# Output projection of a gated two-branch layer, in Strassen's form over four row tiles

## The chip, the cores and the metric

The kernel runs on one core of one Trainium2 chip. The metric is device time in microseconds of one execution, taken as the median over runs. Of the core's engines, PE does the matrix products, DVE, ACT and POOL work on whole rows of elements, and SP issues the transfers between DRAM and the on-chip memory (SBUF). Products are summed in PSUM, which holds eight banks of 512 float32 columns on 128 partitions. Each engine runs its own list of instructions in order; a semaphore is what one engine waits on for another.

## The reference

One layer on 1024 positions of width 1024. What matters here is the middle of it:

```python
merged = (sigmoid(g_a) * (y_att @ w_oa) + sigmoid(g_b) * (y_sgu @ w_ob))
x = x + merged @ w_out
x = x + conv_gated_mlp(rmsnorm(x, ffn_norm), w_up, conv_w, conv_b, w_down)
```

`g_a`, `g_b` are columns of the layer's input projection, `y_att` and `y_sgu` the two branches (attention and spatial gating, 512 wide each), `w_out` is 1024 x 1024, and the MLP projects up to 2 x 2816 columns, filters along the positions, gates, and projects down.

## The kernel before, in words

Everything is kept transposed: features on partitions in tiles of 128, positions along the free axis, whose halves are `L` (0 to 511) and `H` (512 to 1023). Each float32 operand of a product is split into a high part of PE's reduced-precision float32 type and the remainder; a product of two operands is three matmuls (high by high, high by low, low by high). The high part is written by ACT (`copy_hi`, L77), the remainder by DVE or POOL as a subtraction.

The program from the gates on is written out by hand: the order of the calls is the order of the instructions on every engine. Its stages:

1. **Gates** (`gate_pair`, one call for each of 8 column tiles). Both gate tiles of one number are four blocks, and their product by the normalized input is done in Strassen's form: seven products of 12 matmuls (`Blocks.prod`, L928 before, L933 after) for eight. `Left` holds the weight side of a pair: `load_p`, `load_q` fetch it, `sum_s1` to `sum_s4` add blocks on POOL, `split_p`, `split_q`, `split_s3`, `split_r` make high and low parts (`ph`, `pl`, `qh`, `ql`, `s3h`, `s3l` and `AX` in the trace). Beside the gates, `sums_step` makes in advance two sums of blocks of the MLP's up weights: load, two DVE additions (`ls`), store to DRAM. Loads run one step ahead through two buffers.
2. **Branches** (`branch`, 16 jobs of 24 matmuls into `po`). A job's result is multiplied with tanh values that come back from DRAM (`th`), the two branches are added to `m`, and `m_split` makes its parts. Ten more sums steps sit here. `run_jobs` runs all jobs: it issues the matmuls of job i, starts the weight load of job i+4, splits the weights of job i+2 (`wjh` by ACT, `wjl` by POOL), and then runs the rest of job i. `wjh` and `wjl` have two buffers each.
3. **Output projection** (`out_tile`, 8 jobs of 48 matmuls into `px`, one for each tile of 128 features of the result). After a job: the residual is added (`ac`, L1244), scaled rows `h` are made (L1246), `x2` goes to DRAM for the end of the program, and the blocks that the MLP's Strassen form needs (`B11`, `T1`, `B21`, `B22`, `T3`) are split tile by tile; `T2` and `T4` are kept raw. Squares are summed in `sq2` for the second norm.
4. **MLP**, 22 pairs of up columns (`first_pair`, then `fast_pair`), each seven products of 12 matmuls, with the filter and the gate of the pair before on DVE and ACT. The second norm's statistics (`ssq_cols`, 16 matmuls of 2 columns) are made in the first pair, and its row factor `rstd_b` (`rms_rows`, 4 matmuls of 512 columns) in the second, since it scales the results and not the operands. The down projection (`mlp`) is Strassen's form again, one product M at a time over four row tiles: the sums `X` and `Z` stay in PSUM, and a finished one is read out between products.

PSUM tiles of 1024 columns are handed out in rotation from four places (`PS`); a tile's place is free again when its last reader is done, and a wait covers the whole tile, not its halves.

## Time and profile before

| | |
|---|---|
| median of 3 runs (lowest, highest) | 1202.59 us (1201.78, 1203.99) |
| the profiled execution's own time | 1202.22 us |
| its span, first to last instruction | 1200.4 us |
| PE, DVE, ACT, POOL busy in the span | 99%, 74%, 45%, 47% |
| mean granted TensorE clock | 0.997 |

A span is the time from the first to the last recorded instruction. A matmul's record ends when its result is out, so records of neighbours overlap: 389 ns for one of 512 columns, while the next one starts 0.227 us after it. "Idle before" is time in which an engine had nothing running just ahead of an instruction, and the name after the arrow is what ended it.

### The profile page before, as it was taken

To read this page: it belongs to the slowest core of one execution; us is meant where nothing else is said; L and a number is where in the kernel's file an instruction comes from. 1 tells how busy PE (TensorE), PEld (TensorE's weight loads), DVE (VectorE), ACT (ScalarE), POOL (GpSimd) and SP (SyncE) were. 2 spreads that over 40 slices of the span, in tenths; PEclk is the share of its full clock that TensorE was granted. 3 is DMA by queue.
4 is the path that set the end of the run, shared out by engine and by line. 5 is a ranking of instruction groups with operands and counts; after the bars stand their busy time and mean duration, and the time that the engine had idled before them with its cause. 6 is when DMAs were issued, how large, how long until landed. Compare 5 with 4: busy or idle time off the path is not lost.

```text
span 1200.4 us, 15782 instructions
## 1 busy us (share of the span) xinstructions
PE 1183.8 (99%) x5850; PEld 1000.2 (83%) x5850; DVE 886.7 (74%) x1019; ACT 540.5 (45%) x839; POOL 569.3 (47%) x361
## 2 busy tenths in 40 slices
PE   8999999999999999999999999999999999999998
PEld 8889989888888888888788888888888888888886
DVE  7688966755648665668797878878887798866674
ACT  8456566744335222234444444344444445434331
POOL 2366684587768322344856665756666551000000
PEclk9999999999999999999999999999999999999999
DMA  7110133127686997342142333324333358965471
GB/s 274 31 53 19 54 124 131 36 100 244 244 313 212 351 323 270 134 158 106 45 150 88 123 116 121 127 91 143 105 132 107 104 200 273 395 227 193 151 237 60
DMA packets 78989, 191.01 MB, mean 159 GB/s; under 512 B 8896, under 2 KB 9152, under 8 KB 78912
## 3 DMA queue, kind: packets, MB, share of 16 engines
q1 hardware_dynamic: 78912, 190.00, 45.6%
q8 instruction: 46, 0.75, 0.3%
q14 instruction: 31, 0.25, 0.1%
HBM read 139.38 MB, written 50.59 MB: 158 GB/s over the span
## 4 chain that ended last, share of the span: by engine, by line
PE 87%; DVE 5%; ACT 1%; DMA 1%; issue 1%; POOL 0%; SPq 0%; ACTq 0%; DVEq 0%
PE pz L928 45%; PE pd L1634 10%; PE pdy L1634 7%; PE px L82 2%; PE po L83 2%; PE po L82 2%; PE px L83 2%; PE px L81 2%; PE po L81 2%; PE pvs L81 1%; PE pvs L83 1%; PE pvs L82 1%; PE pq L81 1%; PE pq L83 1%; PE pq L82 1%; DMA ls<-wup 1%
## 5 line engine op out<-in xcount | busy, mean ns | idle before, releaser
L928 PE MATMUL pz<-T,qh 128*128 128x512 f32 x480 | 148.0, 389 | 0.0
L887 POOL TENSOR_TENSOR pl<-lp,ph 128x1024 fp32r<-128x1024 f32 x30 | 72.9, 2430 | 86.3 <-ACT ph L77 86.1
L928 PE MATMUL pz<-B,ph 128*128 128x512 f32 x352 | 109.5, 392 | 0.0
L928 PEld LDWEIGHTS pz<-T,qh 128*128 128x128 f32 x480 | 90.0, 188 | 18.6
L928 PE MATMUL pz<-T,ql 128*128 128x512 f32 x240 | 93.4, 389 | 0.0
L98 POOL TENSOR_TENSOR wjl<-wj,wjh 128x512 fp32r<-128x512 f32 (+1 forms) x24 | 40.8, 1701 | 95.5 <-ACT wjh L77 95.5
L887 POOL TENSOR_TENSOR ql<-lq,qh 128x1024 fp32r<-128x1024 f32 x29 | 74.7, 2574 | 9.1 <-ACT qh L77 9.1
L928 PEld LDWEIGHTS pz<-B,ph 128*128 128x128 f32 x352 | 65.4, 188 | 15.5 <-ACT x L1482 1.9
L943 DVE TENSOR_TENSOR pz<-pz,rstd_b 128x1024 f32<-128x1024 f32 x60 | 73.9, 1232 | 4.6 <-ACT rstd_b L132 2.6
L887 POOL TENSOR_TENSOR s3l<-s,s3h 128x512 fp32r<-128x512 f32 x30 | 40.7, 1358 | 72.4 <-ACT s3h L77 72.4
L928 PE MATMUL pz<-T,s3h 128*128 128x512 f32 x240 | 73.9, 389 | 0.0
L928 PE MATMUL pz<-B,pl 128*128 128x512 f32 x176 | 68.6, 390 | 0.0
L1634 PE MATMUL pd<-bh,ah 128*128 128x512 f32 x176 | 68.5, 389 | 0.0
L1634 PE MATMUL pd<-bh,al 128*128 128x512 f32 x176 | 68.5, 389 | 0.0
L1634 PE MATMUL pd<-bl,ah 128*128 128x512 f32 x176 | 68.5, 389 | 0.0
L928 PE MATMUL pz<-T,AX 128*128 128x512 f32 x264 | 65.1, 397 | 0.0
L928 PE MATMUL pz<-B,AX 128*128 128x512 f32 x264 | 63.4, 389 | 0.0
L928 PEld LDWEIGHTS pz<-T,AX 128*128 128x128 f32 x264 | 50.6, 192 | 10.7
L928 PEld LDWEIGHTS pz<-B,AX 128*128 128x128 f32 x264 | 49.5, 188 | 10.3
L1340 DVE SCALAR_TENSOR_TENSOR tg<-pz,cp,tg 128x1023 f32<-128x1023 f32 (+1 forms) x44 | 56.2, 1278 | 0.8
L1340 DVE SCALAR_TENSOR_TENSOR tv<-pz,cp,tv 128x1023 f32<-128x1023 f32 (+1 forms) x44 | 56.2, 1277 | 0.8
L77 ACT ACTIVATE qh<-lq 128x1024 fp32r<-128x1024 f32 (+1 forms) x31 | 32.0, 1036 | 54.5 <-issue 25.4
(331 smaller groups left out, 3523.8 us busy)
## 6 DMA issues: line engine op xcount, KB each, us to landing
ls<-wup SPq DMA_DIRECT2D x22, 512.0 KB, 5.5
sum<-ls SPq DMA_DIRECT2D x22, 512.0 KB, 4.6
lp<-wup SPq DMA_DIRECT2D x22, 512.0 KB, 3.6
ra<-wdown SPq DMA_DIRECT2D x44, 256.0 KB, 4.8
b<-T SPq DMA_DIRECT2D x44, 256.0 KB, 3.9
B<-tv SPq DMA_DIRECT2D x33, 256.0 KB, 2.0
T<-tt SPq DMA_DIRECT2D x33, 256.0 KB, 2.0
b<-B SPq DMA_DIRECT2D x33, 256.0 KB, 3.9
```

What stands on the lines that cost most here:

```text
L77: return nc.scalar.activation(dst, src, AF.Copy, scale=scale)
L81: nc.tensor.matmul(out, wh, mh, start=first, stop=False, **kw)
L82: nc.tensor.matmul(out, wh, ml, start=False, stop=False, **kw)
L83: nc.tensor.matmul(out, wl, mh, start=False, stop=last, **kw)
L98: nc.gpsimd.tensor_tensor(l[:, :nk, :], r[:, :nk, :], h[:, :nk, :].bitcast(F), op=ALU.subtract)
L887: nc.gpsimd.tensor_tensor(l, r, h.bitcast(F), op=ALU.subtract)
L928: nc.tensor.matmul(o, p[:, k, :], y[:, q, k, :], start=not more and k == 0 and j == 0, stop=k == 3 and j == 2, skip_group_check=True)
L943: nc.vector.tensor_tensor(z, z, rstd_b, op=ALU.mult)
L1340: nc.vector.scalar_tensor_tensor(t[:, j:], p[:, 0:1024 - j], cw[:, ci, 2 - j:3 - j], t[:, j:], op0=ALU.mult, op1=ALU.add)
L1634: nc.tensor.matmul(o[d], p[:, k - k0, m], q[:, k - k0, :], start=new and k == 0 and j == 0, stop=k == HK - 1 and j == 2, skip_group_check= ...
```

## The change

`w_out` and the merged rows are each taken as four blocks, and the output projection becomes seven products M1, M2, M6, M5, M3, M7, M4, each over four row tiles and all of K = 512. A product is two groups (`out_group`) of 24 matmuls, so 14 groups take the place of the 8 tiles. `X` and `Z` are two PSUM tiles each, four row tiles of 512 columns. M1 is computed into `X` and copied to `Z`; M6, M5, M3 go on adding to `X`, M2 to `Z`; then M7 starts `Z` anew and M4 adds to it. The quarters of the result are `C11` (Z after M2), `C21` (X after M6, and Z after M4), `C22` (X after M5, and Z after M7) and `C12` (X after M3).

The sums of blocks of `w_out` are made in the gates' stage in eight steps of four DVE additions of 256 columns (`osum_step`), stored to DRAM (`wS`) and read back by the groups. `step` runs these eight first, then the 22 sums of the MLP: two steps in the first gate pair that had none, three in each later pair (two before), and one in each of the first ten branch jobs.

The merged rows stay whole in `m`, and their blocks `mB11`, `mB21`, `mB22`, `mT1` to `mT4` are summed and split after the branches and between the groups (`out_work`). The quarters' own work stands there too: adding the residual (`rows_add`), scaling (`rows_done`), splitting (`right_split`), squaring into PSUM and adding up (`squares`). The scaled rows no longer hold the first norm's factor. `first_pair` has its products in another order, leaves the statistics to the second pair, and takes its PSUM tiles where `X` was.

```diff
     def job_load(i):
         if i < len(jobs):
             src, nk, _ = jobs[i]
-            job_w[i] = wload(src, "wj", nk) if nk else first_left()
-            if not nk:
+            if nk == "g":
+                job_w[i] = raw("wj")
+                nc.sync.dma_start(job_w[i].rearrange("p (a b) m -> p a (b m)", a=2), src())
...
+    def osum_load(i):
+        if i < 8:
+            k, e = divmod(i, 2)
+            x = osum[i] = pools["ls"].tile([128, 4, 256], F, tag="ls", name=nm("os"), bufs=2)
+            for j in range(2):
+                nc.sync.dma_start(x[:, 2 * j:2 * j + 2],
+                                  a["wout"][:, k + 4 * j, :].rearrange("p (r m) -> p r m", r=2)
+                                  [:, :, 256 * e:256 * e + 256])
+        else:
+            sums_load()
+
+    def osum_step(i):
+        osum_load(i + 1)
...
+        sub(nc.vector, x[:, 3], x[:, 3], x[:, 1], ALU.add)
+        sub(nc.vector, x[:, 1], x[:, 0], x[:, 1])
+        sub(nc.vector, x[:, 0], x[:, 3], x[:, 0])
+        sub(nc.vector, x[:, 2], x[:, 2], x[:, 0])
+        nc.sync.dma_start(wS[:, :, k, 256 * e:256 * e + 256], x)
...
         gate_out(("b", c - 1), prev.zg)
-        if c > 1:
-            sums_step()
+        step()
         q.prod(q.v0, "S3", "T3")
...
         if nx:
             nx.sums_r()
-        if c > 1:
-            sums_step()
+        step()
         q.prod(q.v0, "A22", "T4", more=True)
...
+        if c > 1:
+            step()
         q.prod(q.v1, "S2", "T2")
         q.sums(x1, x7, q.v0)
...
-            if n % 2 == 0 or n in (5, 9):
-                sums_step()
+                block_split("B11" if c < 4 else "B21", slice(c % 4, c % 4 + 1), m[:, L].unsqueeze(1))
+                if c > 3:
+                    lo = ms[0][:, c - 4, :]
+                    sub(nc.vector, lo[:, L], lo[:, H], lo[:, L])
+                    sub(nc.vector, lo[:, H], m[:, H], lo[:, H])
+            if sums["make"] < NPAIR:
+                step()
...
+    def out_work(i):
+        hu = hx2["u"] if "u" in hx2 else None
+        if i == 0:
+            block_half("B22", 1, H)
+        if i == 1:
+            for d in range(4):
+                nc.scalar.copy(Z[d], X[d])
+            for k in range(0, 4, 2):
+                sub(nc.vector, ms[1][:, k:k + 2, H], ms[1][:, k:k + 2, H], ms[0][:, k:k + 2, L])
+            block_half("T2", 1, H)
+        if i == 2:
+            block_half("T1", 0, L)
+            block_half("T3", 0, H)
+        if i == 3:
+            rows_add("C11", Z)
+            for k in range(0, 4, 2):
+                sub(nc.vector, ms[1][:, k:k + 2, L], ms[1][:, k:k + 2, L], ms[1][:, k:k + 2, H])
+            block_half("T4", 1, L)
+        if i == 4:
+            hu = hx2["u"] = U("hu", F, [128, 2, 4, 512])
+            rows_done("C11", hu[:, 0])
+            right_split("B11", hu[:, 0], nc.gpsimd)
+            squares("C11", Z)
+        if i == 5:
+            rows_add("C21", X)
+        if i == 6:
+            rows_load("C12")
+        if i == 7:
+            rows_add("C22", X)
+        if i == 9:
+            rows_add("C12", X)
+            rows_done("C12", hu[:, 1])
+            right_sum(hu[:, 0], hu[:, 1], hu[:, 0])
+            right_split("T1", hu[:, 0], nc.gpsimd)
+            squares("C12", X)
+        if i == 11:
+            hc = pools["hc"]
+            rows_add("C22", Z)
+            rows_done("C22", hc)
+            right_split("B22", hc, nc.gpsimd)
+            right_sum(hu[:, 1], hc, hu[:, 1])
+            right_sum(hu[:, 0], hc, hu[:, 0])
+            right_split("T3", hu[:, 1], nc.vector)
+        if i == 12:
+            lefts[0].split_s3()
+            lefts[0].sums_r()
+            lefts[0].split_r(0)
+            right_split("T2", hu[:, 0], nc.vector)
+            squares("C22", X)
+        if i == 13:
+            lefts[0].split_q()
+            rows_add("C21", Z)
+            rows_done("C21", hu[:, 1])
+            right_split("B21", hu[:, 1], nc.vector)
+            right_sum(pools["hc"], hu[:, 1], hu[:, 0])
+            right_split("T4", pools["hc"], nc.vector)
...
+            o = Z if s in ("M2", "M7", "M4") else X
+            y = mb[RHS[s]]
+            for k in range(2):
+                for d in range(4):
+                    for j, (p, q) in enumerate(((0, 0), (0, 1), (1, 0))):
+                        nc.tensor.matmul(o[d], w[p][:, 4 * k + d, :], y[:, q, k0 + k, :],
+                                         start=s in ("M1", "M7") and k0 + k == 0 and j == 0,
+                                         stop=k0 + k == 3 and j == 2, skip_group_check=True)
             yield
...
+            out_work(i)
+        jobs.append((lambda: out_src(s, k0), "g", main))
```

In `squares`, ACT writes the square of a row tile into the PSUM half `o[d]`, and DVE adds that half to `sq2`. `first_pair` now runs A11 B11, S3 T3, S4 B22, S1 T1, S2 T2, A12 B21, A22 T4; `fast_pair`, for the second pair, runs A11 B11, then `ssq_cols`, S1 T1, `rms_rows`, and the rest.

How the change places the instructions, at three places. In the rows `wjh` and `wjl` are the parts of a job's weights, `mB`, `mT` blocks of the merged rows (`mB_623` is B22, `mT_627` T2, `mT_631` T1, `mT_632` T3, `mT_636` T4), `px_4923` and `px_4924` the two tiles of X, `px_4925` and `px_4926` those of Z.

ACT at the start of the projection, as it was (the work after the first two tiles):

```order
L77 ACTIVATE wjh_4926<-wj_4717 128x1024 [waits DMAHW6_49,PE_49,Pool_49]
L77 ACTIVATE B_616_4778<-h_4931 128x512 [waits DVE_49]
L77 ACTIVATE T_617_4779<-h_4931 128x512 [waits DVE_49]
L1263 ACTIVATE sq_4785<-ac_4871 128x1024
L77 ACTIVATE wjh_4993<-wj_4756 128x1024 [waits DMAHW0_49,PE_49,Pool_49]
```

and as it is now (after groups 0 and 1, which are M1):

```order
L77 ACTIVATE wjh_4968<-wj_4781 128x1024 [waits DMAHW7_49,PE_49,Pool_49]
L77 ACTIVATE mB_623_4972<-m_4219 128x1024 x2
L77 ACTIVATE wjh_5003<-wj_4816 128x1024 [waits DMAHW0_49,PE_49,Pool_49]
L1309 COPY px_4925<-px_4923 128x512
L1309 COPY px_4925<-px_4923 128x512 [waits Activation_49]
L1309 COPY px_4926<-px_4924 128x512 [waits PE_49]
L1309 COPY px_4926<-px_4924 128x512 [waits Activation_49]
```

The copies from X to Z are new, and they stand behind the split of the weights of group 3 (`wjh_5003`), which waits until PE has done group 1.

DVE around one tile, as it was (the work after the last tile but two and the last but one):

```order
L612 TENSOR_TENSOR T2f<-h_5288,h_5215 128x512
L612 TENSOR_TENSOR T4f<-h_5288,T2f 128x512 [waits DVE_49]
L1266 TENSOR_TENSOR sq_4785<-sq_4785,px_5231 128x1024 [waits Activation_49]
L1244 SCALAR_TENSOR_TENSOR ac_5225<-px_5304,ac_5225 128x1024 [waits DMAHW4_49,DMAHW3_49,PE_49]
L1246 SCALAR_TENSOR_TENSOR h_5358<-ac_5225,cp,rstd_b 128x1024 [waits DVE_49,Pool_49]
```

and DVE now, from the sums of T4 (after the residual of `C11` was added) to the second reading of X:

```order
L612 TENSOR_TENSOR m_4219<-m_4219 128x2x512 x2
L1218 TENSOR_TENSOR mT_636_5094<-m_4219,mT_636_5094 128x1024 [waits Activation_49] x2
L1282 TENSOR_TENSOR sq_4841<-sq_4841,px_4925 128x512 [waits Activation_49]
L1282 TENSOR_TENSOR sq_4841<-sq_4841,px_4926 128x512 [waits DVE_49,Activation_49]
L1282 TENSOR_TENSOR sq_4841<-sq_4841,px_4926 128x512 [waits Activation_49]
L1265 SCALAR_TENSOR_TENSOR C_4932<-px_4923,C_4932 128x512 [waits DMAHW5_49,PE_49]
L1265 SCALAR_TENSOR_TENSOR C_4932<-px_4923,C_4932 128x512 [waits DMAHW6_49]
```

A tile's sum was read once, and the next tile had another place. Now X is read for `C21` (`C_4932`) and then added to again, and this reading stands behind the squares of `C11`; M5's first matmul waits for DVE.

ACT at the end of the projection, as it was (the last two tiles):

```order
L1265 ACTIVATE px_5231<-ac_5152 128x1024 [waits PE_49]
L77 ACTIVATE ph_5353<-lp_5203 128x1024 [waits DMAHW7_49,PE_49,Pool_49]
L77 ACTIVATE B_616_4778<-h_5358 128x512 [waits DVE_49]
L77 ACTIVATE T_617_4779<-h_5358 128x512 [waits DVE_49]
L1265 ACTIVATE px_5304<-ac_5225 128x1024 [waits PE_49]
```

and as it is now (from the work after group 11 on):

```order
L1271 ACTIVATE hc<-C_4937,cp 128x512 [waits DVE_49] x4
L77 ACTIVATE B_665_5415<-hc 128x512 [waits Activation_49] x4
L77 ACTIVATE T_4839<-hu_5129 128x512 [waits DVE_49] x4
L77 ACTIVATE ph_5464<-lp_5367 128x1024 [waits DMAHW5_49,PE_49,Pool_49]
L77 ACTIVATE s3h_5468<-s_659_5369 128x512 [waits DMAHW6_49]
L77 ACTIVATE AX_5475<-lr_5472 128x1024 [waits Pool_49]
L77 ACTIVATE T_672_5478<-hu_5129 128x512 [waits DVE_49] x4
L1281 ACTIVATE px_4923<-C_4937 128x512
L1281 ACTIVATE px_4923<-C_4937 128x512 [waits DVE_49]
L1281 ACTIVATE px_4924<-C_4937 128x512
L1281 ACTIVATE px_4924<-C_4937 128x512 [waits DVE_49]
```

The first split of the MLP's first weights (`ph`) waited for the last tile but one, which 48 matmuls followed. Now it waits for group 12, which 24 matmuls follow, and it stands behind the splits of B22 and T3. The squares of `C22` in the tiles of X (`px_4923`, `px_4924`) stand behind it, behind `AX` and behind T2.

260 lines of the change are left out of this document (113 added, 147 removed).

## The prediction

> **What bounds the kernel now.** I read the page's totals first, then PE's own waits, then the table of stages, and then the timeline where the change stands.
>
> ```profile
> span 1200.4 us, 15782 instructions
> PE 1183.8 (99%) x5850; PEld 1000.2 (83%) x5850; DVE 886.7 (74%) x1019; ACT 540.5 (45%) x839; POOL 569.3 (47%) x361
> ...
> PE pz L1313 <- DVE sq L1433: 1.8, 1, 1.8
> PE sc L426 <- DVE sm L466: 1.1, 1, 1.1
> ...
> 385.00:472.00 87.00, 87.00 (x385) 72.05 (x384) 54.99 (x55) 19.88 (x25) 28.07 (x18) 1.00 0.86 310
> 472.00:559.10 87.10, 87.10 (x386) 72.10 (x385) 60.52 (x51) 26.74 (x34) 31.97 (x17) 1.00 0.39 142
> 559.10:587.00 27.90, 26.13 (x115) 21.25 (x114) 22.80 (x22) 14.55 (x20) 22.06 (x10) 0.94 0.20 69
> ```
>
> PE is the bound: 99% busy, and its longest single wait of the whole run is 1.8 us. In the last three rows (span, then PE, PEld, DVE, ACT, POOL, the granted clock, DMA's share and GB/s) it never stops in the branches (385 to 472) and in the output projection (472 to 559.1). So a matmul taken away there is worth its full pace, but any new wait of PE is lost in full as well: nothing idle covers it.
>
> ```profile
> L81 PE MATMUL px<-mh,wjh x128: 389/389/389, 472.1 to 558.4; 128*128 128x512 f32 x128
> ...
> L83 PE MATMUL px<-mh,wjl x128: 389/389/389, 472.5 to 558.9; 128*128 128x512 f32 x128
> ```
>
> These are the first and last starts of the projection's 3 x 128 = 384 matmuls: (558.9 - 472.1) / 383 = 0.227 us each. A group of 24 takes 5.44 us, a product of 12 takes 2.72 us.
>
> **The change part by part.** *The product.* 14 groups of 24 are 336 matmuls, 48 fewer: 48 x 0.227 = **-10.9 us**. Everything else is whether DVE, ACT and POOL keep up, since every sum is now read, split or copied between groups of 5.44 us, where a tile had 10.9. Their prices:
>
> ```profile
> 542.01 1.15 ACT L77 ACTIVATE B<-h 128x512 fp32r<-128x512 f32 x2 [3.58 <-DVE h L1246]
> 548.24 1.06 ACT L77 ACTIVATE ph<-lp 128x1024 fp32r<-128x1024 f32 x1 [2.98 <-issue]
> 568.46 0.57 ACT L1429 COPY xu<-pz 128x512 f32<-128x512 f32 x1
> 570.83 1.12 ACT L1432 ACTIVATE px<-ac 128x512 f32<-128x512 f32 x2
> 583.62 1.06 ACT L77 ACTIVATE qh<-lq 128x1024 fp32r<-128x1024 f32 x1 [9.69 <-POOL lr L612]
> ...
> 549.38 2.39 POOL L887 TENSOR_TENSOR pl<-lp,ph 128x1024 fp32r<-128x1024 f32 x1 [4.55 <-ACT ph L77]
> 566.74 2.81 POOL L887 TENSOR_TENSOR AX<-lr,AX 128x1024 fp32r<-128x1024 f32 x1 [3.45 <-ACT AX L77]
> 570.07 6.12 POOL L1418 TENSOR_TENSOR T<-T4f,T 128x1024 fp32r<-128x1024 f32 x2 [0.51 <-ACT T L77]
> 578.92 1.28 POOL L887 TENSOR_TENSOR s3l<-s,s3h 128x512 fp32r<-128x512 f32 x1
> ...
> 548.96 1.22 DVE L1244 SCALAR_TENSOR_TENSOR ac<-px,ac 128x1024 f32<-128x1024 f32 x1
> 557.73 0.68 DVE L1285 SCALAR_TENSOR_TENSOR ac<-px,ac 128x512 f32<-128x512 f32 x1
> 564.54 0.69 DVE L1223 TENSOR_TENSOR B<-h,B 128x512 fp32r<-128x512 f32 x1
> 567.64 6.33 DVE L1418 TENSOR_TENSOR T<-T2f,T 128x1024 fp32r<-128x1024 f32 x2 [0.36 <-ACT T L77]
> ```
>
> ACT: about 0.55 us for 512 columns in a row of several, 1.06 for 1024. DVE: 0.69 and 1.22. POOL: 1.28 and 2.4. Where DVE and POOL both work from SBUF they take turns: from 566.74 to 576.2 POOL did three of 2.4 and DVE two of 1.22, together 9.6 us in 9.5. DVE reading PSUM (548.96, with POOL busy from 549.38) keeps its 1.22. ACT's row at 583.62 shows that an engine keeps its order: it stood 9.69 us behind POOL, and all that came after it too.
>
> Let group 0 start at 0. *M2's start.* M2 adds to Z, so it waits for the copies from X. They stand behind the split of group 3's weights, which waits for group 1 (10.9): split to 12.0, copies of both halves of the first tile to 13.3 (0.57 and a hand-over each). PE stands 2.4 us; 1.7 if one half were enough. I take **+2.4**; group 3 ends at 24.2 instead of 21.8.
>
> *M5's start.* M5 adds to X after DVE has read it for C21. In DVE's order that comes after the three square sums of C11, which come last in this chain: C11's four additions after group 3 (DVE, 2.8; they queue behind T1's and T3's splits, in turns with the weight splits on POOL, to 29.6), T4's two sums (2.4), high parts (1.06 for the last) and remainder (1.22): 37.3. Then ACT scales C11 (2.2), splits B11 (2.2) and squares (1.7): 43.5; two DVE sums, the last square, its sum: 45.9; two additions into C21: 47.3. Group 5 ends at 35.1, so PE stands 12.2 us. The floor is the same links with DVE free and no turns lost: 17.7 us, begun 1.2 before group 3 ends (the first tile of Z is complete then), against two groups of PE's work: 17.7 - 1.2 - 10.9 = 5.6. I take **+10.5**, nearer the upper end because the rows at 566 to 576 show full turns.
>
> *The clock after it.*
>
> ```profile
> 559.10 0.62 PE L928 MATMUL pz<-B,ph 128*128 128x512 f32 x2
> ...
> 574.63 1.95 PE L1313 MATMUL pz<-ones,sq 128*128 128x2 f32 x16 [1.77 <-DVE sq L1433]
> 576.44 4.59 PE L928 MATMUL pz<-T,AX 128*128 128x512 f32 x12
> 580.87 0.63 PE L928 MATMUL pz<-T,qh 128*128 128x512 f32 x2
> 586.33 1.88 PE L130 MATMUL pz<-diag,ones 128*128 128x512 f32 x4
> 587.64 1.03 PE L928 MATMUL pz<-B,ph 128*128 128x512 f32 x2
> ...
> 578.00:580.00 2.00, 2.00 (x6) 1.52 (x6) 1.10 (x2) 0.00 (x0) 2.00 (x2) 0.51 0.00 0
> ```
>
> After 1.77 us of waiting and sixteen tiny matmuls the granted clock was 0.51, and 12 matmuls took 580.87 - 576.44 = 4.43 us for 2.72. So a long wait costs **+1.7** more (0 to 1.7). For the waits of 2 to 4 us the rows leave it open: 1.1 us of waiting (L426) left the clock full, 1.77 with tiny matmuls did not; I take nothing for them and keep 1.7 each for the range. The Trainium skill, page "TensorE: Matmul & The Clock Gate", section "What's actually happening", halves the clock after an idle window of about 3.4 us and gives it back after as much sustained work. By that rule M2's wait stays free and M5's costs the 1.7; were 1.8 us enough, as the row by itself could be read, the sum would be 3.4 higher.
>
> *M3's start* waits for C22's reading of X, with DVE free by then: two additions from 1.2 before the group's end, **+0.3**.
>
> *M4's start.* Z must be read for C22 (after group 11), and group 12's weights be split; ACT does both C12's scaling, T1's parts and squares after group 9 first. Counted from group 9's end: weights' high part of group 11 1.2, scaling 3.3, then sums, T1's parts and POOL's remainders in turns, squares and their last sum 12.3; group 12's weights: high part 12.6, remainder 15.0. The third matmul needs it, and group 11 ends at 10.9: 15.0 - 0.45 - 10.9 = 3.7. Without turns 0.3. I take **+3.2**.
>
> *The first pair.* Its first product writes a PSUM tile where X was, and may not before DVE has added up the squares of C22. ACT and POOL reach them by one chain: `ph` waits for group 12 (1.06), POOL `pl`, `s3l` and two sums `lr` (2.4 + 3 x 1.28 = 6.2), ACT `AX` (1.06), T2's four parts (2.2), then square, sum, square, square, sum, square, sum (about 5): 15.5, while PE has only group 13's 5.44 left. So PE stands at least 10 us. Upper end: turns. From group 13's weight remainder, 4.1 after group 11, POOL has 2.4 + four remainders of B22 5.1 + 6.2 + `AX` 2.4 and DVE 16 times 0.65 for eight sums, T3 and T2: 26.6 us on one port, and 4.3 for squares: 35.0 after group 11's end, where group 13 ends at 14.6. That is 20. I take **+17**, since what is serial on the port is most of it. B21 and T4 follow with 13.6 us of PE's work before them, in time.
>
> *The rest of the first two pairs.* Eight products to 587.64 took 28.5 us for 21.8: 6.8 for the wait, tiny matmuls, slow clock and `rms_rows`. All but the wait is still there, and the power on POOL for the new place stands behind `AX`, some 2 us: **0** (-3 to +2).
>
> *Gates and branches.*
>
> ```profile
> 361.50 4.19 DVE L612 TENSOR_TENSOR ls<-ls 128x512 f32<-128x512 f32 x2 [3.20 <-DMA ls<-wup]
> 381.25 4.00 DVE L612 TENSOR_TENSOR ls<-ls 128x512 f32<-128x512 f32 x2
> ...
> 392.13 0.62 ACT L77 ACTIVATE wjh<-wj 128x512 fp32r<-128x512 f32 x1
> ...
> 392.83 1.29 POOL L98 TENSOR_TENSOR wjl<-wj,wjh 128x512 fp32r<-128x512 f32 x1 [0.58 <-ACT wjh L77]
> ...
> 395.90 0.39 PE L81 MATMUL po<-ah,wjh 128*128 128x512 f32 x1
> ...
> DMA packets 13803, 42.26 MB, mean 291 GB/s; under 512 B 1521, under 2 KB 1521, under 8 KB 13795
> ```
>
> Twenty steps now stand where there were twelve. Most hide: in the windows' row of the branches DVE has 32 us free, and PE's pairs run ahead of DVE by a pair's PSUM. The last gate pair does not hide its third step: it comes between DVE's step at 381.25 and the sums that end in the last tanh, and POOL is splitting `ya` there, so it takes 4 us too. The tanh is followed on ACT by `wjh` at 392.13 and on POOL by `wjl` to 394.1, which the third matmul after 395.90 (at 396.35) needs: 2.2 of slack, so 4.0 - 2.2 = 1.8. With a load as late as that before 361.50 (3.2) it is about 5; with the loads early and short turns, nothing. I take **+2** (0 to 6). Loads and stores of the projection itself (512 KB a group, asked for four groups ahead, where the row of that stage shows DMA at 0.39), and those at the program's end, cost 0: they are off every chain named here.
>
> The sum: -10.9 + 2.4 + 10.5 + 1.7 + 0.3 + 3.2 + 17 + 0 + 2 = **+26.2 us**. On the profiled execution's 1202.2 (its span and 1.8 around it, 0.4 below the median shown) that is **1228 us**. All lower ends together give -10.9 + 1.7 + 5.6 + 0 + 0.3 + 0.3 + 10 - 3 + 0 = +4, all upper ones +37 and 3.4 for the clock.
>
> **The rivals.** *DVE and POOL hardly wait for each other*, because their operations seldom meet: M5's wait goes to 6, M4's to 0.7, the pair's to 11, and the sum to -10.9 + 2.4 + 6 + 1.7 + 0.3 + 0.7 + 11 + 2 = +13, 1215 us. For it: the projection's row has POOL busy for 32 of 87 us only. Against it: fourteen weight splits of 2.4 and twelve remainders of 1.28 make 49 us in 76. The Trainium skill, page "SBUF — State Buffer", section "SBUF: two separate sides", calls the port shared by DVE and GpSimd an exclusive lock held for a whole instruction. It agrees with the 9.5 us at 566 to 576, and leaves open who goes first.
>
> *Transfers bind the first ten branch jobs.* They now hold a step each: 512 KB of tanh, 256 of weights and 768 + 512 of the step in 5.44 us are 385 GB/s, where the last row above gives 291 from 330 to 475 and the stage's row 310. At 310 a job would take 6.8, ten of them 13 us more: 1241 us. Against it: PE has four PSUM tiles of lead and loads go out four jobs ahead, and the six jobs behind have no step.
>
> *Not slower.* If `ph` finds a free buffer when group 11 ends, and not group 12, the chain to the first pair begins 5.44 us earlier, under PE's work, and the pair waits 4.6 instead of 10; with the other terms at their lower ends -10.9 + 1.7 + 5.6 + 0.3 + 0.3 + 4.6 - 3 = -1.4, 1201 us. It decides where the pair waits under 6 us and M5 does too. Against it: `wjh` has two buffers, and group 13 holds the other; and in ACT's order four parts of B22 and four of T3 stand ahead of `ph`, of which the last needs sums that come 11 us or so after group 11.
>
> **How the numbers follow.** Forecast 0.63 (1221 to 1236 by itself), little waiting between DVE and POOL 0.16, transfers 0.1, not slower 0.11, of which just under half ends within 0.2%, about what a measurement of this kernel can tell from no change. So faster 0.06, same 0.05, slower 0.89. The range reaches from below the second case to just short of the third: 1210 to 1240 us.
>
> **What would show it.** In the changed kernel PE's waits, none above 1.8 us before, should read: about 2.4 for ACT's copy (L1309) at M2, 10 for DVE's residual of C21 (L1265) at M5, 3 at M4 (POOL's `wjl` or DVE), 17 for DVE's square sum (L1282) ahead of the first pair's first product; the granted clock near 0.5 after the long ones; and the projection's matmuls 336. Should DVE's square sums of C11 end near group 5's end, M5's step is wrong; should PE reach the first pair within 6 us of group 13, the pair's is. A branch stage above 90 us would speak for the transfers.

## The result, and the profile after

The changed kernel takes **1280.84 us** (median of 4 runs, 1276.20 to 1284.56), the kernel before 1202.18 (4 runs, 1200.69 to 1203.99): 1.0652 times as long, 95% interval 1.0606 to 1.0697, or 78.7 us more. The prediction said 1228, in a range of 1210 to 1240. The direction was right; the loss is three times as large as forecast.

The page of the changed kernel (totals), and PE's own waits: who it waited for, us in total, times, the longest.

```profile
span 1282.9 us, 15839 instructions
PE 1203.1 (94%) x5802; PEld 1006.2 (78%) x5802; DVE 938.0 (73%) x1084; ACT 565.0 (44%) x886; POOL 587.0 (46%) x371
...
PE pz L933 <- ACT x L1104: 16.1, 5, 4.0
PE pz L933 <- DVE sq L1282: 12.9, 2, 12.1
PE px L1371 <- DVE C L1265: 10.7, 1, 10.7
PE po L81 <- ACT wjh L77: 7.2, 4, 2.3
PE pz L933 <- ACT xt L1481: 7.0, 1, 7.0
PE po L83 <- POOL wjl L98: 4.3, 7, 0.6
...
PE px L1371 <- ACT px L1309: 2.1, 1, 2.1
PE px L1371 <- ACT wjh L77: 1.9, 1, 1.9
```

PE was 99% busy and is 94% busy. The waits for `C` (L1265), for `px` (L1309) and, in the last row, for `wjh` stand in the projection and were forecast (10.5, 2.4 and 3.2). The first row stands in the gates and the two of `po` in the branches; for both stages together the forecast had 2 us.

The table of stages: gates, branches, projection, and the first pairs; columns as before (span, then PE, PEld, DVE, ACT, POOL, the granted clock, DMA's share, GB/s). First the changed kernel:

```profile
225.00:409.60 184.60, 167.84 (x715) 136.44 (x714) 129.18 (x124) 72.82 (x97) 118.89 (x65) 0.94 0.66 218
409.60:515.10 105.50, 93.94 (x385) 73.21 (x384) 62.20 (x63) 16.07 (x25) 28.21 (x18) 0.97 0.80 273
515.10:614.20 99.10, 83.62 (x337) 66.78 (x335) 63.46 (x57) 48.20 (x66) 53.54 (x27) 0.90 0.42 145
614.20:690.00 75.80, 52.20 (x195) 40.15 (x196) 47.12 (x56) 31.19 (x46) 31.51 (x18) 0.80 0.18 62
```

and the gates of the kernel before, which the prediction did not show:

```profile
225.00:385.00 160.00, 158.93 (x720) 131.41 (x721) 97.17 (x93) 74.67 (x99) 117.83 (x65) 1.00 0.60 207
```

The borders are the first and last matmuls of a stage. From them the whole loss comes out, stage by stage:

| stage | before, us | after, us | difference | forecast |
|---|---|---|---|---|
| gates, up to the branches' first matmul | 385.0 | 409.6 | +24.6 | } +2 |
| branches | 87.1 | 105.5 | +18.4 | } |
| projection, first to last start | 86.8 | 98.7 | +11.9 | +7.2 |
| from there to the down projection's first matmul | 427.1 | 455.5 | +28.4 | +17 |
| the rest of the span | 214.4 | 213.6 | -0.8 | 0 |

(The forecast for the projection is -10.9 + 2.4 + 10.5 + 1.7 + 0.3 + 3.2.) The sum is 82.5 us, the difference of the two spans, 1282.9 and 1200.4. More than half of it, 43.0, lies ahead of the projection.

### The profile page after: what moved, and what is told of

It is laid out like the page before. It is cut to its first block, busy times and chain, and to the rows that moved or that the text cites. A ratio compares the mean times of both kernels' runs of the same rounds, so it can differ in the third digit from the quotient of the medians.

```text
span 1282.9 us, 15839 instructions
## 1 busy us (share of the span) xinstructions
PE 1203.1 (94%) x5802; PEld 1006.2 (78%) x5802; DVE 938.0 (73%) x1084; ACT 565.0 (44%) x886; POOL 587.0 (46%) x371
## 4 chain that ended last, share of the span: by engine, by line
PE 67%; DVE 13%; DMA 9%; ACT 3%; issue 2%; SPq 1%; POOL 1%; DVEq 0%; ACTq 0%
PE pz L933 36%; PE pd L1693 9%; PE pdy L1693 7%; DMA sum<-ls 6%; PE px L1371 3%; DMA ls<-wup 2%; DVE ls L612 2%; DVE hu L612 1%; DVE os L612 1%; PE pvs L81 1%; PE pvs L83 1%; PE pvs L82 1%; DVE mT L1218 1%; PE pq L81 1%; DVE T L1289 1%
## 5 line engine op out<-in xcount | busy, mean ns | idle before, releaser
L98 POOL TENSOR_TENSOR wjl<-wj,wjh 128x512 fp32r<-128x512 f32 (+1 forms) x30 | 55.2, 1842 | 125.8 <-ACT wjh L77 115.1
L892 POOL TENSOR_TENSOR pl<-lp,ph 128x1024 fp32r<-128x1024 f32 x30 | 72.9, 2430 | 82.6 <-ACT ph L77 82.5
L612 DVE TENSOR_TENSOR ls<-ls 128x512 f32<-128x512 f32 x44 | 47.2, 1075 | 42.3 <-DMA ls<-wup 32.8
L933 PE MATMUL pz<-x,ph 128*128 128x512 f32 x128 | 46.3, 447 | 16.3 <-ACT x L1104 16.1
L933 PEld LDWEIGHTS pz<-T,s3h 128*128 128x128 f32 x240 | 46.0, 192 | 17.0 <-ACT xt L1481 7.5
L77 ACT ACTIVATE wjh<-wj 128x512 fp32r<-128x512 f32 (+1 forms) x30 | 24.6, 826 | 77.9 <-DMA wj<-wob 21.6
L933 PEld LDWEIGHTS pz<-B,AX 128*128 128x128 f32 x264 | 49.9, 189 | 10.5
```

The costliest lines, as they stand in the source:

```text
L77: return nc.scalar.activation(dst, src, AF.Copy, scale=scale)
L98: nc.gpsimd.tensor_tensor(l[:, :nk, :], r[:, :nk, :], h[:, :nk, :].bitcast(F), op=ALU.subtract)
L612: eng.tensor_tensor(out, x, y, op=op)
L892: nc.gpsimd.tensor_tensor(l, r, h.bitcast(F), op=ALU.subtract)
L933: nc.tensor.matmul(o, p[:, k, :], y[:, q, k, :], start=not more and k == 0 and j == 0, stop=k == 3 and j == 2, skip_group_check=True)
```

## The experiments

Each is an edit of the changed kernel, unless the text says otherwise. Single runs stand beside a run of the kernel before on the same chip; they are read by their stages, and only the last three, which were timed in rounds, by a ratio.

### What delays PE in the gates

The timelines of DVE, ACT and PE in the changed kernel, around the sums of one gate pair (start, length, line, operation; in brackets idle time ahead of it and what ended it):

```profile
281.52 10.28 DVE L612 TENSOR_TENSOR os<-os 128x256 f32<-128x256 f32 x8 [0.38 <-DMA os<-wout]
291.71 0.69 DVE L941 TENSOR_TENSOR pz<-x,pz 128x512 f32<-128x512 f32 x1
...
292.49 0.59 ACT L942 COPY u<-pz 128x512 f32<-128x512 f32 x1 [8.41 <-DVE pz L941]
295.84 1.02 ACT L1015 ACTIVATE th<-pz 128x1024 f32<-128x1024 f32 x1 [2.76 <-DVE pz L948]
296.76 0.58 ACT L1104 COPY x<-pz 128x512 f32<-128x512 f32 x1
...
297.39 1.22 PE L933 MATMUL pz<-x,ph 128*128 128x512 f32 x2 [3.44 <-ACT x L1104]
```

The second and the third step of a pair stand in a row on DVE (eight additions of 256 columns, 10.28 us), ahead of the pair's sums (L941). The sums end in a tanh on ACT (L1015), and behind that tanh, in ACT's order, stands `x1`, the copy of the *next* pair's first product (L1104). PE adds A12 B21 onto that product and waits 3.44 us. It does so in five pairs, 16.1 us in all, and the granted clock of the stage falls to 0.94. The edit leaves out the third step of a gate pair:

```diff
-        if c > 1:
-            step()
         q.prod(q.v1, "S2", "T2")
         q.sums(x1, x7, q.v0)
```

The steps that are left over go into the last six branch jobs.

> Edit: the third step of a gate pair is left out, and all sixteen branch jobs hold a step instead of the first ten (30 steps as in the change). Theory A (the second and third step stand in a row on DVE ahead of the pair's sums, the tanh and the next pair's copy x1 are late by them, and PE stands at A12 B21 in five pairs): the five waits on ACT x L1104, 16.1 us in the change, fall under 3 us, the granted clock in the gates is back at 1.00, and the branches begin at 385 to 391 us instead of 409.6. Theory B (the new loads and stores, 1 KB pieces, bind the gates by themselves): the branches still begin after 400. For the branches, theory A (a step there takes 6.6 us of load, store and two buffers, whatever else happens) expects 16 x 6.6 = 106 us for the stage, as against 105.5 with ten steps and the late start; whole time 1255 to 1264 us.

Measured: 1268.53 us (before 1200.93). PE's waits on this copy are 0.5 us in all, and the branches begin at 384.9. Theory A holds for the gates: without the third step all of the 24.6 us are back, clock included. Theory B falls: the loads and stores in 1 KB pieces are all still there, though spread over more pairs. The branches took 100.0 us, less than the 106 expected, though with sixteen steps. The whole time missed its range (1255 to 1264), since the projection took 113.2: PE now waits 10.4 us for the split weights there (2.6 in the changed kernel), and in SP's queue their loads stand behind those of the steps.

What was not tried apart is how much of the steps' delay is DVE's turns with POOL and how much late loads. In the pair shown the loads were in time (0.38 us of waiting), and the additions were long: one of 256 columns took 0.416 us at least and 0.949 in the median. In later pairs the loads were late as well: DVE waited 17.6 us in all for `ls` in the gates of the changed kernel, 5.9 in this one and 5.6 in the kernel before.

### What delays PE in the branches

SP's queue and DVE in the changed kernel, over two of the branch jobs:

```profile
434.89 0.33 SPq L961 DMA_DIRECT2D ls<-wup  x1
...
441.52 0.33 SPq L961 DMA_DIRECT2D ls<-wup  x1
...
442.44 0.36 SPq L975 DMA_DIRECT2D sum<-ls  x1
...
443.33 0.98 SPq L87 DMA_DIRECT2D wj<-woa  x1
449.40 0.33 SPq L961 DMA_DIRECT2D ls<-wup  x1
...
440.35 1.42 DVE L612 TENSOR_TENSOR ls<-ls 128x512 f32<-128x512 f32 x2 [1.36 <-DMA ls<-wup]
...
SPq L961 <- DMA sum<-ls: 35.6, 9, 5.1
```

A buffer that is loaded at 434.89 is added up at 440.35, stored at 442.44, and loaded again at 449.40, when the store has landed (the last line: SP waited 35.6 us for such stores in the stage, in nine steps). That is 14.5 us a round, over two buffers 7.25 a step, where PE needs 5.44 a job. A job's own weights (`wj`, at 443.33) are asked for behind such a load (441.52) in SP's queue, and so they come late too. The edit of the changed kernel: a pool of four buffers for the steps in the branches, in space that the gates leave free, and loads two steps ahead.

```diff
-            x = pools["ls"].tile([128, 3, 4, 128], F, tag="ls", name=nm("ls"), bufs=2)
+            x = pools["l2" if deep else "ls"].tile(..., bufs=4 if deep else 2)
...
         for key in B_ORDER[:2]:
             th_load(key)
+        sums_load()
```

> Edit: in the branches the steps load into four buffers instead of two, and loads run two steps ahead; the bytes moved are the same. Theory L (a loop of latencies: load 6.4 us, additions 1.4, store 5.7 until the buffer is free, over two buffers = 6.7 us a job where PE needs 5.44): the steps come every 5.5 us, the waits of DVE's ls on its load go, and the branches take 88 to 95 us instead of 105.5; whole time 1267 to 1274 us. Theory T (bytes: 2 MB a job at 300 GB/s are 6.7 us): the stage stays at 100 to 106 us and the whole time at 1276 to 1285. The gates and all behind the branches are as in the change in both.

Measured: 1270.9 us (before 1200.93); the branches take 91.1 us, the gates are unchanged. Theory L holds. The transfers run faster with the same bytes; one stretch of this kernel's branches:

```profile
440.00:450.00 10.00, 10.00 (x46) 8.29 (x45) 7.71 (x10) 1.90 (x3) 2.78 (x3) 1.00 1.04 417
```

417 GB/s in this stretch, and 316 in the mean of the stage, where the changed kernel moved 273. Theory T, and the second rival of the prediction with it, took some 300 for a ceiling, and it was none. The kernel before showed that already: in slices of 2.2 us of its branches the rate goes up to 425. But with four buffers the transfers are busy all the time (share 1.04 in the row), so there is little room beyond that.

The next kernel has both edits, the one on the gates and the one on the buffers.

> Edit: both of the last two edits on the steps together: two steps in a gate pair, one in each of sixteen branch jobs, four buffers there and loads two steps ahead. Theory A with L (the row of two steps on DVE in the gates, the loop over two buffers in the branches, and no more): the branches begin at 385, take 87 to 92 us, and the projection's weights are in time again (the first matmul of the projection at 472 to 477 us, against 515.1 in the change and 472.1 before); from there on as in the change; whole time 1236 to 1246 us. Rival T (sixteen steps' bytes bind the branches): the stage takes 98 to 104 us, whole time 1250 to 1258.

Measured: 1245.85 us (before 1201.38). The branches, now with sixteen steps, run at PE's full pace:

```profile
387.80:474.80 87.00, 87.00 (x385) 72.07 (x384) 60.76 (x72) 16.90 (x25) 28.56 (x18) 1.00 0.98 383
```

Both edits together take back 40.3 of the 43.0 us (474.8 for 515.1; one wait of 2.1 us on the copy `x1` in the gates is left). Rival T falls again. The counter-test puts the change's steps into the kernel before, and leaves its projection alone:

```diff
-        if c > 1:
-            sums_step()
+        step()
...
+        if c > 1:
+            step()
         q.prod(q.v1, "S2", "T2")
...
-            if n % 2 == 0 or n in (5, 9):
-                sums_step()
+            if sums["make"] < NPAIR:
+                step()
```

> Edit: the kernel before, with the change's thirty steps in the change's places (two or three in a gate pair, one in each of the first ten branch jobs; the eight new sums are stored and not used; they are loaded in pieces of 1 KB as in the change, though from other places of w_out, so the stored values differ), and its own projection and first pair. Theory (the steps alone make the 43 us that the gates and branches lost in the change): the branches begin at 406 to 411 us and the projection at 508 to 516; whole time 1238 to 1247. Rival (part of it comes from the sums of merged rows and from block splits in the branches, or from w_out's new layout): the projection begins before 502, whole time under 1234.

Measured: 1242.48 us (before 1201.38). The projection begins at 512.4, 40.3 us later than before: the thirty steps in these places make 40.3 of the 43.0 us lost ahead of the projection, without any Strassen product in it behind them.

### The waits on X and Z in the projection

The squares of C11 go behind DVE's reading of X:

```diff
         if i == 4:
             rows_done("C11", hu[:, 0])
             right_split("B11", hu[:, 0], nc.gpsimd)
-            squares("C11", Z)
         if i == 5:
             rows_add("C21", X)
+            squares("C11", Z)
```

> Edit: the squares of C11 stand behind DVE's reading of X for C21 (after group 5 instead of group 4). Theory A (M5's start waits for that reading because it stands behind the squares): the wait of 10.7 us at M5 falls to 1 to 3 us, the clock stays at 1.00 there, and the projection, 98.7 us from the first to the last start in the change, takes 83 to 88 us; whole time 1265 to 1273. Rival (DVE is late by its other work, T4's sums and remainders): the wait stays above 7 us, whole time above 1274.

Measured: 1272.8 us (before 1200.93). PE's wait on DVE's reading of X (L1265) falls from 10.7 to 4.0 us in two pieces, the projection from 98.7 to 89.2. Theory A holds for the mechanism and falls a little short in size (1 to 3 us and 83 to 88 were expected). 3.5 us of waiting for POOL's weight remainders (`wjl`) appeared instead.

### Ahead of the MLP's first pair

The first two products of the first pair in the changed kernel, DVE's work ahead of them, and ACT's copy `x1` (L1481):

```profile
626.31 1.22 PE L933 MATMUL pz<-B,ph 128*128 128x512 f32 x2 [12.15 <-DVE sq L1282]
638.31 1.22 PE L933 MATMUL pz<-T,s3h 128*128 128x512 f32 x2 [7.01 <-ACT xt L1481]
...
600.16 15.04 DVE L612 TENSOR_TENSOR hu<-hc,hu 128x512 f32<-128x512 f32 x8
615.13 9.18 DVE L1289 TENSOR_TENSOR T<-hu,T 128x512 fp32r<-128x512 f32 x8
624.23 0.68 DVE L1282 TENSOR_TENSOR sq<-sq,px 128x512 f32<-128x512 f32 x1
...
635.40 2.38 ACT L77 ACTIVATE T<-hc 128x512 fp32r<-128x512 f32 x4 [1.67 <-DVE hc L612]
637.69 0.57 ACT L1481 COPY xt<-pz 128x512 f32<-128x512 f32 x1
```

The wait for the squares is there, 12.15 us. Sixteen DVE operations of some 0.62 us took 24.2, in turns with POOL. Behind it PE waits again, 7.01 us: the second product goes into the other half of the first one's PSUM tile and waits for `x1`, which stands on ACT behind all of C21's scaling and splitting. The first edit takes the squares out of the way:

```diff
             right_split("T2", hu[:, 0], nc.vector)
-            squares("C22", X)
...
         q.prod(q.g1, "S4", "B22")
+        squares("C22", Z)
```

> Edit: the squares of C22 are written to Z's place inside the MLP's first pair instead of X's place ahead of it, so that its first product waits for no square. Theory A (the chain behind it is as late: the copy x1 of the first product stands on ACT behind C21's scaling and the splits of B21 and T4, ending at 635 us in the change): the wait of 12.1 us ahead of the first product falls under 2 us, but the second product still starts only 3 to 7 us earlier than in the change (638.3 there, counted from the last group of the projection: 24.1 us after it; 17 to 21 expected); whole time 1274 to 1280. Rival (the squares are the whole delay): the second product starts within 8 us of the last group, whole time 1258 to 1266.

Measured: 1275.29 us (before 1200.93). PE's waits in this kernel:

```profile
PE pz L933 <- ACT xt L1480: 20.8, 1, 20.8
```

The wait ahead of the first product is gone, and the next product waits 20.8 us. That one starts 23.5 us after the projection's last group, for 24.1 in the changed kernel. The stretch to the down projection is 453.7 us, for 455.5; that is hardly a gain, since three kernels above with the same code there (the gate edit, the buffer edit and both) have 454.7 to 457.8. Theory A holds even more strictly than expected (17 to 21): the squares were not the bound, only the first to be waited for. The next edit also brings `x1` ahead of C21's work:

```diff
         if i == 13:
+            q.prod(q.v1, "A11", "B11")
+            nc.scalar.copy(x1, q.v1)
             lefts[0].split_q()
             rows_add("C21", Z)
```

> Edit: the squares of C22 in Z's place inside the first pair as in the edit before that did so, and besides the pair's first product and ACT's copy x1 of it issued ahead of C21's scaling and splits. Theory (PE stands ahead of the second product for the copy x1, which stands on ACT behind C21's work; once it is ahead, the next bound is T3's remainder on DVE): the second product starts 5 to 9 us after the last group of the projection (24.1 in the change), and of the 18 us so won 8 to 14 are left at the end of the pair, where B21 and T4 are late in their turn; from the projection's last matmul to the down projection's first 442 to 448 us instead of 455.5; whole time 1262 to 1272. Rival (T3 and the weights' sums on POOL are as late as x1): the second product starts 15 us or more after the last group, the stretch stays above 451.

Measured: 1276.12 us (before 1203.93). The second product starts 8.8 us after the last group, as expected, but only 4.5 of the 15.3 us so won are left at the down projection: 451.0 us, at the rival's bound, and the whole time is above the 1262 to 1272 expected. The timeline says where they went:

```profile
619.07 1.22 PE L933 MATMUL pz<-T,s3h 128*128 128x512 f32 x2 [6.06 <-ACT xt L1357]
633.78 3.06 PE L933 MATMUL pz<-T,AX 128*128 128x512 f32 x12 [3.38 <-ACT xt L1485]
640.49 1.22 PE L933 MATMUL pz<-B,ph 128*128 128x512 f32 x2 [3.65 <-DVE pz L1495]
...
597.52 15.06 DVE L612 TENSOR_TENSOR hu<-hc,hu 128x512 f32<-128x512 f32 x8
612.50 11.37 DVE L1289 TENSOR_TENSOR T<-hu,T 128x512 fp32r<-128x512 f32 x8
623.79 2.47 DVE L1265 SCALAR_TENSOR_TENSOR C<-px,C 128x512 f32<-128x512 f32 x4
```

DVE is busy without a gap from C22's sums on, and reaches C21's addition at 623.79, 13.5 us after PE has made C21. So long as DVE's work stays as it is, what follows is late, and the waits only show where PE meets it. The bound here is this row of DVE's, drawn out by its turns with POOL.

### A version with all of it mended

One rework, with the steps as in e5: the products in the order M1 M2 M6 M7 M5 M3 M4, so that X and Z alternate but for one place; copies from X to Z ahead of the weight split, shared by DVE and ACT; squares in SBUF; the first pair's products in another order, with `x1` early.

```diff
-    O_STEPS = ("M1", "M2", "M6", "M5", "M3", "M7", "M4")
+    O_STEPS = ("M1", "M2", "M6", "M7", "M5", "M3", "M4")
...
+            if i == 1:
+                for d in range(4):
+                    (nc.vector.tensor_copy if d % 2 else nc.scalar.copy)(Z[d], X[d])
             yield
```

> Edit: the previous edits on the steps, and the projection in the order M1 M2 M6 M7 M5 M3 M4 (X and Z alternate but for M5 to M3); the copies from X to Z ahead of the weight split, half of them by DVE; the squares of the rows written to SBUF instead of X and Z; the first pair's products in the order A11 B11, S4 B22, S1 T1, S3 T3, S2 T2, A12 B21, A22 T4, the first two issued ahead of C21's work. Theory (the projection's and the pair's losses are all waits of PE on X, Z, x1 and the splits, and the clock after them): the projection takes 77 to 83 us (98.7 in the change, 76.2 at full pace), no wait of PE above 3 us in it, and from its last matmul to the down projection's first 436 to 444 us instead of 455.5; whole time 1200 to 1214 us. Rival (DVE and POOL have too much work for fourteen groups, so the waits come back elsewhere): the projection stays above 88 us or the stretch behind it above 448; whole time above 1220.

Measured: 1234.38 us (before 1201.38), projection 88.6, the stretch behind it 454.9: the rival holds, for both. POOL's `wjl` (5.6 us in three waits) and the squares' sums on DVE, now in turns with POOL (eight in 13.19 us, and 9.1 us of waiting ahead of the statistics), took the places of the old waits.

The second rework against the first, in its core (`XT` are the two PSUM tiles of X):

```diff
-            rows_done("C12", hu[:, 1])
-            right_sum(hu[:, 0], hu[:, 1], hu[:, 0])
+            for d in range(4):
+                nc.scalar.activation(X[d], R2["C12"][:, d, :], AF.Copy, scale=g2[:, d:d + 1])
+            for d in range(0, 4, 2):
+                sub(nc.vector, hu[:, 0, d:d + 2, :], XT[d // 2]..., hu[:, 0, d:d + 2, :])
...
-            nc.scalar.activation(t, R2[n][:, d:d + 2, :], AF.Square)
+            nc.scalar.activation(t[:, d:d + 2, :], t[:, d:d + 2, :], AF.Square)
+        nc.vector.tensor_tensor(t[:, 0:2], t[:, 0:2], t[:, 2:4], op=ALU.add)
...
-        for k in range(4):
+        for k in range(0, 4, w):
-            copy_hi(comb[n][:, 0, k, :], h[:, k, :])
+            copy_hi(comb[n][:, 0, k:k + w, :], h[:, k:k + w, :])
```

> Edit: the rework before, with fewer turns between DVE and POOL (remainders and sums on DVE in pieces of 1024 columns, C12's scaled rows in X's PSUM place so that T1 and T3 are summed from PSUM), the squares written in place and ahead of the second pair's weight splits, T4's block sums a group later, the weights' second split ahead of T3's, and the second pair's A12 B21 ahead of its row factor. Theory (the rework's waits were turns on the port and squares late for the statistics): the projection takes 78 to 84 us (88.8 in the first rework), the wait of 9.1 us ahead of the statistics goes, the stretch from the projection's last matmul to the down projection's first takes 432 to 442 us (454.7 in the first rework, 427.1 before); whole time 1206 to 1222. Rival (port-bound: DVE's and POOL's SBUF work between the last groups and the second pair is more than PE's): the stretch stays above 446, whole time above 1224.

Measured: 1215.18 us (before 1203.93), projection 80.4, stretch 447.0. Fewer and larger DVE operations, and sums read from PSUM, helped the projection as expected. The stretch is the rival's (above 446): the largest wait left in it is one of 11.0 us, for DVE's sum into the first pair's PSUM, behind the squares. The third rework's edit on that, besides the smaller ones that its expectation names:

```diff
+        nc.vector.tensor_tensor(x7, x7, x5, op=ALU.add)
+        nc.vector.tensor_tensor(q.g1, x5, q.g1, op=ALU.add)
         squares("C12")
         squares("C21")
-        nc.vector.tensor_tensor(x7, x7, x5, op=ALU.add)
-        nc.vector.tensor_tensor(q.g1, x5, q.g1, op=ALU.add)
```

> Edit: the second rework, with DVE's sums into the first pair's PSUM ahead of the squares (they stood behind them, and the pair's sixth product waited 11.0 us), the squares of C11 and C22 a group later, the remainders of B11 and B22 on DVE instead of POOL, and the second pair's sums of weights and split of them behind the statistics. Theory (the 11.0 us and the clock behind it were the largest part left): the stretch from the projection's last matmul to the down projection's first takes 429 to 436 us (446.7 in the second rework, 427.1 before), the projection 78 to 81; whole time 1197 to 1206 us, within 0.4% of the kernel before. Rival (the statistics or the second pair's weights are as late): the stretch stays above 440, whole time above 1208.

Measured: 1207.21 us (median of 5) against 1201.09 (8 runs): ratio 1.0056, interval 1.0035 to 1.0077. The projection now takes 77.5 us, and the stretch behind it 439.5, between the theory and its rival, and so is the whole time. Its table of stages, projection and first pairs (its branches take 87.0 us):

```profile
473.30:551.20 77.90, 76.91 (x337) 62.74 (x336) 59.74 (x57) 44.48 (x50) 39.30 (x17) 1.00 0.60 212
551.20:615.00 63.80, 53.37 (x219) 41.49 (x219) 51.76 (x51) 34.88 (x43) 31.61 (x16) 0.95 0.26 86
```

The fourth rework moves three things (only their new places are shown):

```diff
+            for d in range(0, 4, 2):
+                sub(nc.vector, hu[:, 1, d:d + 2, :], pools["hc"][:, d:d + 2, :], XT[d // 2]...)
             right_split("T1", hu[:, 0], nc.vector)
...
+        nc.vector.tensor_tensor(q.g1, x5, q.g1, op=ALU.add)
+        nc.vector.tensor_tensor(x7, x7, x5, op=ALU.add)
         for d in range(0, 4, 2):
             sub(nc.vector, pools["hc"][:, d:d + 2, :], hu[:, 1, d:d + 2, :], hu[:, 0, d:d + 2, :])
...
         nc.scalar.copy(x7, q.v0)
+        if rms:
+            prev.tap_g()
+            prev.conv()
```

> Edit: the third rework, with DVE's two sums into the first pair's PSUM ahead of T4's sum and remainder (the sixth product waited 3.5 us), T3's sum ahead of T1's remainder (the first product waited 1.0), and in the second pair ACT's copy x7 ahead of the filter's second tap (the product behind it waited 2.4). Theory (each of these waits and the slow clock after the two longer ones is PE's loss in full): the waits of 3.5 and 2.4 us fall under 1.2, the clock stays full behind them, the stretch from the projection's last matmul to the down projection's first takes 429 to 434 us (439.5 in the third rework, 427.1 before); whole time 1196 to 1203 us, 0.994 to 1.002 of the kernel before. Rival (T4 or the second pair's x7 is late by what goes ahead now): the stretch stays above 436, whole time above 1204.

Measured: ratio 1.0084 (1.0066 to 1.0102; medians 1213.40 and 1202.08), the stretch 448.6: the rival. T3's sum ahead of T1's remainder put four DVE remainders, of 1.2 us each where they have no neighbour, in one row with four pieces of POOL's (2.41, 3.39, 2.29 and 3.33 us):

```profile
549.47 12.31 DVE L1300 TENSOR_TENSOR T<-hu,T 128x1024 fp32r<-128x1024 f32 x4
```

The fifth takes the first of the three back:

```diff
-            for d in range(0, 4, 2):
-                sub(nc.vector, hu[:, 1, d:d + 2, :], pools["hc"][:, d:d + 2, :], XT[d // 2]...)
             right_split("T1", hu[:, 0], nc.vector)
```

> Edit: the fourth rework without its change to T3's sum (which stands behind T1's remainder again, as in the third). Theory (that change alone put four remainders of DVE in one row with four pieces of POOL, 12.3 us, and cost the fourth rework its gain; the other two edits do what was expected of them): the waits of 3.5 and 2.4 us of the third rework are under 1.2, the stretch from the projection's last matmul to the down projection's first takes 429 to 435 us; whole time 1198 to 1204 us, 0.996 to 1.003 of the kernel before. Rival (DVE's sums ahead of T4 make T4 or the next pair's weights late): the stretch stays at 437 us or more, whole time above 1205.

Measured: ratio 1.0063 (1.0044 to 1.0081; medians 1210.05 and 1203.07), the stretch 445.5: the rival again, so the undone change alone had not cost the gain. The row of 12.31 is gone, and the two waits that the other edits aimed at are indeed under 1.2. But now the second pair's first weights are late (`ph` on ACT, 2.2 us, and `pl` on POOL, 2.5), because ACT's squares stand ahead of them, and in the third pair the copy of the first product is (`x`, L1567, 2.7). No version beat the kernel before. In the best one by its median, the third (the fifth's interval overlaps with its own), the projection is 9.3 us shorter (86.8 to 77.5) of the 10.9 that the fewer matmuls promise; behind it 12.4 us are lost, and 1.2 ahead of it. Whether an order exists in which DVE, ACT and POOL hide the last quarter's work stays open.

## Why the prediction was wrong, point by point

**The gates.** The step "most hide ... PE's pairs run ahead of DVE by a pair's PSUM" failed. PE does not run ahead by a pair: it meets ACT's copy `x1`, which stands behind the tanh of the pair before. The third step was costed in the last pair only (+2 for all); in fact it stands ahead of the sums on DVE in each of the six pairs that have one. The kernel before showed how little room there was in that place, and where there was more:

```profile
DVE pz L936 <- PE pz L928: 7.6, 5, 4.7
DVE x L1092 <- PE pz L928: 41.0, 6, 9.0
```

Ahead of these sums DVE waited for PE 7.6 us in five pairs, 4.7 of it in one, so mostly under 1 us a pair. A third step of 4 to 5 us did not fit there. Measured: 24.6 us, with the clock. The second row is DVE's wait at the sum of `x7`, which stands ahead of the second step: 41.0 us in six pairs. A third step ahead of that sum would have met idle time. Whether it would be hidden there, and its load in time, was not tried.

**The branches.** "DVE has 32 us free" was true and beside the point. The forecast failed in taking the loads and stores for hidden; 18.4 us were lost, and 14.4 of them come back with four buffers (105.5 to 91.1). The rival on transfers came near that (13 us more in ten jobs), but by luck: it divided the bytes by 310 GB/s, a rate that was no ceiling. What bound was the round of load, addition and store through two buffers. The page of the kernel before had both parts of it in its list of transfers (a size in KB, then us from issue to landing):

```profile
ls<-wup SPq DMA_DIRECT2D x22, 512.0 KB, 5.5
sum<-ls SPq DMA_DIRECT2D x22, 512.0 KB, 4.6
```

5.5 + 4.6 + 1.4 for the additions make 11.5 us a round and 5.75 a step even at these lighter loads, and PE needs 5.44 a job. With a step in ten jobs out of sixteen this had been hidden; with a step in each of ten in a row it could not be.

**The projection** went by its steps: -10.9 for the matmuls is nearly reached by the best rework (-9.3 with 0.9 us of waiting left); M5's wait was 10.7 for 10.5, M2's 2.1 for 2.4, M4's 1.9 and 0.7 for 3.2. Only the clock was mis-sized. What is left of the stage without its matmuls at full pace and without the waits is 98.7 - 76.2 - 15.4 = 7.1 us, where 1.7 stood; the granted clock was near 0.5 behind the waits at M2, M5 and M4 alike, for 3 us or more each time.

**The first pair.** The wait ahead of its first product was 12.15 for 17, but not because the turns between DVE and POOL were shorter than taken: the last square sum of C22 ended 31.2 us after group 11, where the forecast had 14.6 + 17 = 31.6. The product did not wait for that one. It started at 626.31, when the two sums that read its own tile were done and two more were to come, some 2 us earlier; and group 13 ended 17.0 us after group 11 instead of 14.6, by the slow clock. "B21 and T4 follow ... in time" held, with PE as late as it was: their last remainders ended at 634.7 and 639.5, their products began at 652.05 and 654.77. What failed is "the rest of the first two pairs: 0". The forecast asked when the operands would be ready, not what stood ahead of the copy `x1` in ACT's order, which was C21's work (7.01 us of waiting). The statistics' `diag` (2.68) and smaller waits came behind, and the clock with them. Of 23.6 us of waits in the stretch (12.15 + 7.01 + 0.77 + 2.68 + 1.02) the kernel before had 1.8; the other 6.6 of its 28.4 us are left for the slow clock, granted 0.80 in the stage's row.

**The rivals.** Little waiting between DVE and POOL: wrong, sums and remainders took 24.2 us for 10. Transfers: right in place, wrong in mechanism. Not slower: wrong.

**The range** reached to 1240 because gates and branches had 0 to 6 us in it. A mechanism that repeats in every pair and job was priced once. But the rest was too small as well: with gates and branches mended the kernel still took 1245.85 us.

## What to carry to other kernels

Work that is "off the critical path" has a place in an in-order queue: ask in every round, not only in the last, what stands behind it on its own engine, and follow that through the next engine's order until a PE instruction. The room is what the engine waited just there before (7.6 us in five pairs), not its idle share of the stage. A load, compute, store round through n buffers gives one step in (load + compute + store) / n; compare that with PE's time for a job before calling a transfer hidden, and add buffers before blaming bytes. Where DVE and POOL took turns, many small operations of DVE (sixteen of 0.62 us) lost to POOL's larger ones (24.2 us for 10). And taking away the wait that PE shows first only moved it, unless the work behind it got shorter.

## What the runs showed of the hardware

Waits of some 2 us can slow the clock. In the changed kernel the wait of 2.06 us at M2's start, which ended at 528.20, was followed by a half clock (windows of 2 us, columns as in the tables of stages):

```profile
528.00:530.00 2.00, 1.80 (x4) 1.49 (x5) 2.00 (x1) 1.97 (x4) 1.69 (x1) 0.53 0.00 0
530.00:532.00 2.00, 2.00 (x7) 1.54 (x6) 2.00 (x3) 1.28 (x2) 0.00 (x0) 0.61 0.59 147
532.00:534.00 2.00, 2.00 (x11) 1.61 (x9) 1.12 (x1) 0.00 (x0) 0.00 (x0) 1.00 0.30 123
```

and in the third rework a wait of 2.41 us that ended at 598.50 left the clock full for a little over a microsecond, and then it was half:

```profile
598.00:600.00 2.00, 1.50 (x6) 1.28 (x7) 1.97 (x3) 1.41 (x2) 1.81 (x2) 0.95 0.00 0
600.00:602.00 2.00, 2.00 (x6) 1.52 (x6) 1.76 (x2) 0.74 (x1) 2.00 (x2) 0.50 0.00 0
602.00:604.00 2.00, 2.00 (x8) 1.58 (x7) 1.65 (x2) 1.35 (x2) 1.92 (x2) 0.69 0.00 0
```

What the clock lacks in these windows is (0.47 + 0.39) x 2 = 1.7 us of work in the first case and (0.05 + 0.50 + 0.31) x 2 = 1.7 in the second, so each slow stretch lasts some 3.4 us at half clock. The length of the wait alone does not decide it: in the branches of the changed kernel one of 2.08 us left the clock at 1.00 in every window up to 430.

```profile
422.72 0.50 PE L81 MATMUL po<-ah,wjh 128*128 128x512 f32 x1 [2.08 <-ACT wjh L77]
...
424.00:426.00 2.00, 1.92 (x8) 1.61 (x9) 0.00 (x0) 0.00 (x0) 1.27 (x2) 1.00 0.99 291
```

Single waits of 1.0 and 1.2 us in the third rework left it at 1.00, too. The Trainium skill, page "TensorE: Matmul & The Clock Gate", section "What's actually happening", names an idle window of about 3.4 us as what halves the clock, and lets that window run freely. The length of the slow stretches agrees with it; the threshold does not: here 2.06 us of idle were enough once, and 2.08 were not another time. The prediction had weighed just that rule for M2's wait and taken no loss.

The other: the transfers held 417 GB/s over 10 us with four buffers for the steps, where the mean of the same stage was 310 in the kernel before and 273 in the changed one.
